# All three branch gates as Strassen products with the tokens stationary and 512 weight columns moving

## Chip, cores and metric

The kernel runs on one core of a Trainium2 chip. The metric is the device time of one execution in microseconds, the median of three runs.

## What is computed

One layer of a streaming encoder on 512 tokens of width 1024, all in float32. The change lies between the attention branches and the output projection:

```python
proj = u @ w_in[l]            # u = rmsnorm(h), 512 x 1024
(gq, gk, gv, gg, ga, fq, fk, fv, ff, mq, gates) = split_cols(proj, PROJ_SIZES)
...
y_gla = o_gla.reshape(B, S, GLA_V) @ w_gla_o[l]
...
y_fox = o_fox.reshape(B, S, FOX_W) @ w_fox_o[l]
...
y_mem = o_mem.reshape(B, S, MEM_W) @ w_mem_o[l]
gt = jax.nn.sigmoid(gates.reshape(B, S, N_BRANCH, D))
merged = gt[:, :, 0] * y_gla + gt[:, :, 1] * y_fox + gt[:, :, 2] * y_mem
h = h + merged @ w_out[l]
```

Each gate is a product of 512 x 1024 by 1024 x 1024, each branch output one of 512 x 512 by 512 x 1024. Behind them stand the projection by w_out and a squared-ReLU MLP of width 4096.

## The kernel before

**Precision.** Every float32 operand is split into a high and a low part, and a product is three matmuls (`mm3`, L169 to L172): high x high, high x low, low x high. The weights come as chunks of 128x1024 (512 KB) from the array `wst`; `load_w` issues the load on SP into one of three buffers named raw, `split_w` casts it on ACT (hi, L160) and subtracts on DVE (lo, L161), three buffers each. On a matmul line the trace names first what is written, then its two operands.

**Order.** The instructions of PE stand in the order in which the code is written. Independent PE work is interleaved by `weave`: after each step of a stage's own list it takes units, one `mm3` each, from generators that fill the gaps, in proportion to the step's share. Where `in_order()` or `issue_after` stand, the order of ACT, DVE and SP is the written one, too; elsewhere a scheduler sets it.

**Stages.** Front (u, the memory keys and values), then the fox stage (forgetting attention, 96 filler units: projections for gla), the mem stage (cross attention, 64 filler units: `fox_out`, which holds four of the eight tiles of the fox gate and the eight tiles of the fox output), the gla stage (64 filler units: `gla_g`, then `fox_late`, the other four tiles of the fox gate), then the gates of mem and gla by `gate_group`, the projection by w_out, the MLP.

**The fox gate before** is a plain product in feature layout: a tile is 128 channels by 512 tokens, weights stationary, 512 tokens moving, 8 x `mm3` a tile. `acc[j]`, eight tiles of 128 channels by 512 tokens, collects the merged branches.

**mem and gla before** use Strassen's scheme in Winograd's form: 7 products for a 2 x 2 block product in place of 8. The blocks A11 to A22 are u (tokens 0 to 255 or 256 to 511, by the two halves of the inputs). A `gate_group` computes 512 channels by 512 tokens: each product takes a chunk of weights, stationary, and 256 tokens of u or of a sum of u's blocks, moving: 24 matmuls 256 wide. The sums of the weight blocks are built in the tiles wb: two loads on SP (L1066, L1067), and more blocks added on top of them by accumulating DMAs from GpSimd (`plus`, L1073). The sums of u's blocks are made on DVE (`u_sum`, `lefts_1`, `lefts_2`) and split into S1 to S4 (f0, f1, f2 and the half of uhl that is no longer read). PSUM products are combined in the ct tiles (`take`), a tanh on ACT gives the gate, `merge` multiplies by the branch output on DVE (L1129) and adds to acc on GpSimd (L1130). In the group with `last` set, the merged tile is split at once into mh and ml for w_out (L1133).

## Time and profile before

| | |
|---|---|
| time, median of 3 runs | 808.15 us (808.0 to 808.75) |
| span of the profiled execution | 806.1 us |
| chain that ended last | PE 96%, DMA 2% |
| chunk casts on ACT, L160, 128x1024 | 61 from raw, mean 1050 ns; 19 from wb, mean 1049 ns |
| chunk splits on DVE, L161, 128x1024 | 61 from raw, mean 1308 ns; 19 from wb, mean 1283 ns |
| DMA | 161.29 MB, mean 200 GB/s |
| ACT's waits for a wb tile's DMA | 18.5 us in 7 times |

The profiled execution stands 2.05 us below the median. A row of a group reads: line, engine, operation, what is written <- what is read with its shape, count, busy time, mean of one. In a timeline a row begins with its start and its duration in us; a matmul's duration overlaps the next one's, so rates are read from starts. In a table of windows each engine's busy time stands with its number of instructions, then PE's granted clock, the share of time in which the DMA engines were busy, and GB/s.

### The profile page before, as it was taken

The numbers are of one execution on the slowest core, as the hardware profiler recorded it, in microseconds if no ns is written. First come the engines' busy times: TensorE is split into PE (matmuls) and PEld (weight loads), VectorE is DVE, ScalarE is ACT, GpSimd is POOL, SyncE is SP. The second block draws the span as 40 slices with busy tenths as digits, with TensorE's granted clock in tenths as the row PEclk, the third lists the DMA queues.
The fourth block names the chain that finished last, engine by engine and source line by source line (L and its number), as shares of the span: only waits on it lengthen the run. The fifth ranks groups of instructions, "written<-read, shape, count | busy, mean of one in ns | idle before, by whom it ended". The sixth has DMA issues, their size and how long they took to land.

```text
span 806.1 us, 12359 instructions
## 1 busy us (share of the span) xinstructions
PE 797.7 (99%) x4703; PEld 699.4 (87%) x4703; DVE 602.2 (75%) x941; ACT 444.0 (55%) x714; POOL 107.2 (13%) x136
## 2 busy tenths in 40 slices
PE   9999999999999999999999999999999999999996
PEld 7788888888888888999999889988998899889985
DVE  6877878456455677877567558788798779978897
ACT  7867555443344334444354446874667366647764
POOL 0000010011101121143144100011001100100011
PEclk9999999999999999999999999999999999999998
DMA  9355665688788877758758823898758966896644
GB/s 355 141 160 165 188 169 183 206 229 254 206 255 260 213 233 200 187 136 209 197 143 236 262 78 131 282 249 216 246 169 197 222 211 174 187 262 214 167 81 131
DMA packets 39628, 161.29 MB, mean 200 GB/s; under 512 B 4752, under 2 KB 5456, under 8 KB 37200
## 3 DMA queue, kind: packets, MB, share of 16 engines
q1 hardware_dynamic: 28432, 98.34, 34.7%
q0 software_dynamic: 9776, 58.20, 34.6%
q10 hardware_dynamic: 1360, 3.96, 1.5%
q8 instruction: 37, 0.61, 0.3%
q14 instruction: 23, 0.19, 0.1%
HBM read 158.35 MB, written 35.68 MB: 241 GB/s over the span
## 4 chain that ended last, share of the span: by engine, by line
PE 96%; DMA 2%; DVE 0%; ACT 0%; SPq 0%; issue 0%; POOLq 0%; DVEq 0%; POOL 0%; ACTq 0%
PE mm L170 17%; PE mm L171 17%; PE mm L172 17%; PE mm L1276 16%; PE a L171 6%; PE a L170 6%; PE a L172 6%; PE mm L1605 3%; PE mm L1606 1%; DMA xt<-in_xT_dram 1%; PE mm L611 1%; DMA mem_s<-in_memT_dram 1%; PE a L404 1%; PE a L664 1%; PE a L702 1%; PE a L701 1%
## 5 line engine op out<-in xcount | busy, mean ns | idle before, releaser
L161 DVE TENSOR_TENSOR wlo<-raw,whi 128x1024 fp32r<-128x1024 f32 x61 | 79.7, 1308 | 55.8 <-ACT whi L160 55.6
L170 PE MATMUL mm<-uhl,whi 128*128 128x512 f32 (+1 forms) x336 | 119.6, 356 | 0.0
L172 PE MATMUL mm<-uhl,wlo 128*128 128x512 f32 (+1 forms) x336 | 117.5, 350 | 0.0
L171 PE MATMUL mm<-uhl,whi 128*128 128x512 f32 (+1 forms) x336 | 117.3, 349 | 0.0
L160 ACT CAST whi<-raw 128x1024 fp32r<-128x1024 f32 x61 | 64.1, 1050 | 85.5 <-PE mm L171 44.0
L1336 DVE TENSOR_TENSOR lo<-raw,hi 128x1024 fp32r<-128x1024 f32 x52 | 63.5, 1223 | 14.8 <-ACT hi L1335 14.7
L1335 ACT CAST hi<-raw 128x1024 fp32r<-128x1024 f32 x52 | 54.4, 1048 | 36.0 <-PE mm L1276 16.2
L170 PEld LDWEIGHTS mm<-uhl,whi 128*128 128x128 f32 x336 | 63.6, 189 | 9.2 <-issue 1.4
L172 PEld LDWEIGHTS mm<-uhl,wlo 128*128 128x128 f32 x336 | 63.6, 189 | 8.5
L171 PEld LDWEIGHTS mm<-uhl,whi 128*128 128x128 f32 x336 | 63.7, 190 | 7.6
L1276 PE MATMUL mm<-u,hi 128*128 128x256 f32 x384 | 65.1, 283 | 0.0
L1655 POOL DMA_DIRECT2D b<-in_wst_dram x30 | 25.6, 855 | 262.5 <-DVE lo L1336 134.3
L1276 PEld LDWEIGHTS mm<-u,hi 128*128 128x128 f32 x384 | 56.8, 191 | 0.3
L170 PE MATMUL mm<-hi,ch 128*128 128x512 f32 (+1 forms) x132 | 50.9, 386 | 0.0
L171 PE MATMUL mm<-lo,ch 128*128 128x512 f32 (+1 forms) x132 | 50.9, 386 | 0.0
L172 PE MATMUL mm<-hi,cl 128*128 128x512 f32 (+1 forms) x132 | 50.9, 386 | 0.0
L1276 PE MATMUL mm<-u2s,hi 128*128 128x256 f32 x288 | 47.6, 283 | 0.0
L1276 PE MATMUL mm<-u,lo 128*128 128x256 f32 x192 | 47.5, 283 | 0.0
L1335 ACT CAST hi<-b 128x1024 fp32r<-128x1024 f32 x26 | 27.2, 1048 | 29.6 <-PE mm L172 20.2
L1276 PEld LDWEIGHTS mm<-u2s,hi 128*128 128x128 f32 x288 | 41.8, 192 | 0.3
L1336 DVE TENSOR_TENSOR lo<-b,hi 128x1024 fp32r<-128x1024 f32 x26 | 31.7, 1224 | 11.0 <-ACT hi L1335 11.0
L161 DVE TENSOR_TENSOR wlo<-wb,whi 128x1024 fp32r<-128x1024 f32 x19 | 24.4, 1283 | 20.7 <-ACT whi L160 20.7
(448 smaller groups left out, 2104.5 us busy)
## 6 DMA issues: line engine op xcount, KB each, us to landing
raw<-in_wst_dram SPq DMA_DIRECT2D x113, 512.0 KB
raw<-T SPq DMA_DIRECT2D x32, 512.0 KB
b<-in_wst_dram POOLq DMA_DIRECT2D x32, 512.0 KB, 5.7
T<-in_wst_dram POOLq DMA_DIRECT2D x12, 1024.0 KB, 9.1
b<-in_wst_dram SPq DMA_DIRECT2D x16, 512.0 KB
wb<-in_wst_dram POOLq DMA_DIRECT2D x15, 512.0 KB, 5.4
T<-in_wst_dram POOLq DMA_DIRECT2D x12, 512.0 KB, 6.0
wb<-in_wst_dram SPq DMA_DIRECT2D x8, 512.0 KB
```

Source lines behind the costliest of these rows:

```text
L160: cast = nc.scalar.copy(hi, raw)
L161: low_now[0] = nc.vector.tensor_tensor(lo, raw, f(hi), op=ALU.subtract).ins
L170: nc.tensor.matmul(ps, lh, rh, start=start, stop=False, skip_group_check=on)
L171: nc.tensor.matmul(ps, lh, rl, start=False, stop=False, skip_group_check=on)
L172: nc.tensor.matmul(ps, ll, rh, start=False, stop=stop, skip_group_check=on)
L404: nc.tensor.matmul(ps, x[:, k, sl], w[low][:, kk, :], start=k == low == 0 and x is mxh, stop=k == KT - 1 and low == 1)
L611: nc.tensor.matmul(ps, w[0][:, k, :], u[:, k, :], start=k == 0 and u is uhi, stop=False)
L1276: nc.tensor.matmul(ps[:, a, :], x[:, a, k, :], y[:, s, k, :], start=start, stop=stop, skip_group_check=go is not None)
L1335: split_now[0] = nc.scalar.copy(hi, raw).ins
L1336: split_now[1] = nc.vector.tensor_tensor(lo, raw, f(hi), op=ALU.subtract).ins
L1605: nc.tensor.matmul(ps, wh[:, a, k, :], u[:, :, k, :], start=k == 0, stop=False, skip_group_check=True)
L1655: nc.gpsimd.dma_start(to[i], wst[index["B", q, i, x]], accum_op=ALU.add)
```

## The change

All three gates run by the same scheme, in token layout: a PSUM tile is 128 tokens by 512 channels, the u blocks are stationary and 512 weight columns move. A gate of 1024 x 1024 weights is one Strassen product, its blocks 512 x 512, each block two chunks of 256 rows by 512 columns. The seven products run in the order 1, 2, 5, 3, 6, 7, 4, two slots of 12 matmuls each; products 1, 6, 7, 4 go on adding in one pair of PSUM tiles, 5 and 3 in another. The code lists slots and what each slot issues on the other engines (`at`), with each chunk's cast and split two slots ahead of its matmuls (`high`, `low`). The three branch outputs are in token layout, too: fox's go straight into acc (now four tiles of 128 tokens by 1024 channels), mem's into ymem, gla's stay in PSUM (Y slots). The merged tile is turned to feature layout for w_out by 32 transposes on PE (`turn`). The fox gate leaves the mem and gla stages; the fillers there are now the gg projections, gla_k(1), gla_q(1) and the outputs, and the sums of u stand in the mem stage.

```diff
-    for j in range(KT):
-        L.append(("T", "w_in", OFF["gate_fox"] + P * j))
-        if j % 2 == 0:
-            L.append(("O", "w_fox_o", j // 2))
-    for g, o in (("gate_mem", "w_mem_o"), ("gate_gla", "w_gla_o")):
-        for i in range(2):
-            L += [("W", g, i, b) for b in ("11", "12", "21", "22")]
-            L += [("O", o, 2 * i + 1), ("O", o, 2 * i)]
+    for g, o in (("gate_fox", "w_fox_o"), ("gate_mem", "w_mem_o"), ("gate_gla", "w_gla_o")):
+        L += [("N", "w_in", 2 * j, OFF[g] + 512 * c) for c in range(2) for j in range(4)]
+        L += [("N", o, 2 * j, 512 * c) for c in range(2) for j in range(2)]
...
-        weave([partial(fn, i) for fn, i, _ in steps], 96, gla_k(0), fox_pair(2), fox_pair(3), gla_k(1), gla_q(0), gla_q(1), gvg,
+        weave([partial(fn, i) for fn, i, _ in steps], 80, fox_pair(2), gla_k(0), fox_pair(3), gla_q(0), gvg,
...
-    acc = [mp.tile([P, S], F32, name=f"acc{j}") for j in range(KT)]
+    acc = [mp.tile([P, D], F32, name=f"acc{t}") for t in range(NT)]
...
+    def outputs(wo, oh, ol, to):
+
+        for c in range(2):
+            ws = [[x.rearrange("p (k c) -> p k c", k=2) for x in get_w(("N", wo, 2 * j, 512 * c))] for j in range(2)]
+            for t in range(NT):
+                ps = mmt()
+                sl = slice(t * P, t * P + P)
+                for k in range(4):
+                    mm3(ps, oh[k][:, sl], ol[k][:, sl], ws[k // 2][0][:, k % 2, :], ws[k // 2][1][:, k % 2, :], k == 0, k == 3)
+                    if k == 3:
+                        nc.scalar.copy(half_of(to[t], c), ps)
+                    yield
...
+    def u_sum(n):
+
+        x = xsum[n] = xsp.tile([P, 4, 256], F32, tag=f"x{n}", name=f"x{n}")
+        if n == 1:
+            nc.vector.tensor_tensor(x, A21[0], A22[0], op=ALU.subtract)
+            nc.vector.tensor_tensor(x, x, A21[1], op=ALU.add)
+            nc.vector.tensor_tensor(x, x, A22[1], op=ALU.subtract)
+        else:
+            nc.vector.tensor_tensor(x, xsum[1], A11[0], op=ALU.subtract)
+            nc.vector.tensor_tensor(x, x, A11[1], op=ALU.subtract)
...
-        Q, A, T, V_ = (lambda i: run(mem_q(i))), mem_scores, mem_turn, mem_values
-        steps = [(Q, 1), (A, 0), (Q, 2), (T, 0), (A, 1), (V_, 0), (Q, 3), (T, 1), (A, 2), (V_, 1), (T, 2), (A, 3), (V_, 2),
-                 (T, 3), (V_, 3)]
-        weave([partial(*st) for st in steps], 64, fox_out())
+        Q, A, T, V_, U = (lambda i: run(mem_q(i))), mem_scores, mem_turn, mem_values, u_sum
+        steps = [(Q, 1, 0), (A, 0, 4), (Q, 2, 4), (T, 0, 2), (A, 1, 2), (V_, 0, 0), (Q, 3, 2), (T, 1, 3), (A, 2, 5), (V_, 1, 5),
+                 (T, 2, 4), (U, 1, 0), (A, 3, 6), (V_, 2, 5), (U, 2, 0), (T, 3, 6), (V_, 3, 0)]
+        weave([partial(fn, i) for fn, i, _ in steps], 48, gla_g(0, mp, "th"), gla_g(1, mp, "th"),
+              outputs("w_fox_o", ofh, ofl, acc), shares=[n for *_, n in steps])
+    ymp = omst.enter_context(pool("ymem", side="right"))
+    ymem = [ymp.tile([P, D], F32, name=f"ymem{t}") for t in range(NT)]
...
+    def gate_key(g, b, n):
+
+        kh, ch = BLOCK[{1: "11", 2: "21", 3: "22"}.get(b, b)]
+        return "N", "w_in", 2 * (2 * kh + n), OFF[g] + 512 * ch
...
+        def gate_ready(n):
...
-            (u_sum, (3,), 0), (gla_turn, (2,), 3), (gate_ready, ("11",), 0), (gate_ready, ("21",), 0), (gla_turn, (3,), 3))
-        weave([partial(fn, *a) for fn, a, _ in steps], 64, *[gla_g(j) for j in range(4)], fox_late(), shares=[n for *_, n in steps])
+            (gla_values, (0,), 0), (gla_scores, (1,), 8), (gla_turn, (0,), 0), (gla_turn, (1,), 4), (gla_values, (1,), 10),
+            (gate_ready, (0,), 0), (gla_turn, (2,), 6), (gate_ready, (1,), 0), (gla_turn, (3,), 0))
+        weave([partial(fn, *a) for fn, a, _ in steps], 64, gla_k(1), gla_q(1), gla_g(2, lp, "og"),
+              outputs("w_mem_o", omh, oml, ymem), gla_g(3, lp, "og"), shares=[n for *_, n in steps])
...
+        GATES = ("gate_fox", "gate_mem", "gate_gla")
+        ORDER = (1, 2, 5, 3, 6, 7, 4)
+        slots = []
+        for g in range(3):
+            for n in ORDER:
+                if g == 2 and n == 4:
+                    slots += [("Y", 1, 0), ("Y", 1, 1)]
+                slots += [(g, n, 0), (g, n, 1)]
+        slots += [("Y", 0, 0), ("Y", 0, 1)] + [("O", 0, j) for j in (2, 3, 0, 1)]
+        at_slot = {k: i for i, k in enumerate(slots)}
...
+        def load_sum(g, n, other):
+            nc.sync.dma_start(sum_tile(g, n, other), wst[index[gate_key(GATES[g], "12" if other else "11", n)]])
+
+        def plus(g, n, other, b):
+            nc.gpsimd.dma_start(sum_tile(g, n, other), wst[index[gate_key(GATES[g], b, n)]], accum_op=ALU.add)
+
+        def source(key):
+            g, n, c = key
+            return raws[key] if key in raws else sum_tile(g, c, n == 7)
+
+        def high(key):
+            hi, lo = ws[key] = [wp.tile([P, 1024], F32R, tag=x, name=nm(x)) for x in ("hi", "lo")]
+            next_sum(nc.scalar.copy(hi, source(key)).ins)
+
+        def low(key):
+            hi, lo = ws[key]
+            nc.vector.tensor_tensor(lo, source(key), f(hi), op=ALU.subtract)
+            if key[0] not in ("Y", "O") and key[1] in (1, 5, 6) and key[:2] != (0, 1):
+                plus(key[0], key[2], 0, {1: "12", 5: "22", 6: "21"}[key[1]])
+
+        def mms(key):
+            g, n, c = key
+            wh, wl = (x.rearrange("p (k c) -> p k c", k=2) for x in ws[key])
+            uh, ul = GATE[n]
+            if c == 0 and n in (1, 2, 5):
+                cur[n] = [(at_ if n == 2 else mmt)() for _ in range(2)]
+            ps = cur[{1: 1, 6: 1, 7: 1, 4: 1, 2: 2, 5: 5, 3: 5}[n]]
+            for t in range(2):
+                for k in range(2):
+                    kk = 2 * c + k
+                    mm3(ps[t], uh[:, kk, spans[t]], ul[:, kk, spans[t]], wh[:, k, :], wl[:, k, :], n in (1, 2, 5) and kk == 0,
+                        kk == 3, True)
...
+        def evac(ps):
+            tt = pool_.tile([P, S], F32, tag=tag, name=nm("tt"))
+            nc.scalar.activation(tt, ps, AF.Tanh, scale=0.5)
+            nc.vector.scalar_tensor_tensor(sg[j], tt, 1.0, ps, op0=ALU.add, op1=ALU.mult)
+            nc.vector.tensor_scalar(sg[j], sg[j], ghead[:, j:j + 1], 0.5, op0=ALU.mult, op1=ALU.mult)
+        return proj(OFF["gg"] + P * j, evac)
+
+    xsum = {}
+    A11, A12, A21, A22 = ([f(t[:, 4 * k:4 * k + 4, 256 * i:256 * i + 256]) for t in (uhi, ulo)] for i in range(2) for k in range(2))
+
...
+        def merge(g, i, c, ys=None):
+            for t in (2 * i, 2 * i + 1):
+                x, a = th[g, i, c][:, t % 2], half_of(acc[t], c)
+                if g == 0:
+                    nc.vector.scalar_tensor_tensor(a, x, 1.0, a, op0=ALU.add, op1=ALU.mult)
+                else:
+                    nc.vector.scalar_tensor_tensor(x, x, 1.0, half_of(ymem[t], c), op0=ALU.add, op1=ALU.mult)
+                    merged[0] = nc.gpsimd.tensor_tensor(a, a, x, op=ALU.add).ins
...
+        def turn(t, c):
+            pt = (at_ if c else mmt)([P, 4, P])
+            for k in range(4):
+                nc.tensor.transpose(pt[:, k, :], half_of(acc[t], c)[:, k * P:(k + 1) * P], ident)
+            h, l = (x[:, 4 * c:4 * c + 4, spans[t]] for x in (mh, ml))
+            nc.scalar.mul(h, pt, 0.5)
+            nc.vector.scalar_tensor_tensor(l, pt, 0.5, f(h), op0=ALU.mult, op1=ALU.subtract)
+
+        def sum_four():
+            vec(xsum[1], xsum[2], A12[0])
+            vec(xsum[1], xsum[1], A12[1])
+
+        def sum_three():
+            x = xsum[2]
+            nc.vector.scalar_tensor_tensor(x, x, -1.0, A22[0], op0=ALU.mult, op1=ALU.subtract)
+            vec(x, x, A22[1], ALU.subtract)
...
+        for g in range(3):
+            if g:
+                for n in range(2):
+                    at((g - 1, 7, 1), load_sum, g, n, 0, shift=-1)
+                    at((g - 1, 4, 1), load_sum, g, n, 1, shift=-1)
+                    at((g - 1, 4, 1), plus, g, n, 1, "22", shift=-1)
+            for n in (2, 3):
+                for c in range(2):
+                    at((g, n, c), get, (g, n, c), shift=max(-5, -at_slot[g, n, c]))
...
+        at((0, 1, 1), vec, sum_tile(0, 0, 0), sum_tile(0, 0, 0), sum_tile(0, 0, 1), shift=-1)
+        at((0, 1, 1), plus, 0, 0, 1, "22", shift=-1)
+        at((0, 1, 1), left, S1, xsum[1], shift=-1)
+        at((0, 1, 1), vec, sum_tile(0, 1, 0), sum_tile(0, 1, 0), sum_tile(0, 1, 1))
+        at((0, 1, 1), plus, 0, 1, 1, "22")
+        at((0, 5, 0), sum_four)
+        at((0, 5, 1), left, S4, xsum[1])
+        at((0, 3, 0), left, S2, xsum[2])
+        at((0, 6, 0), sum_three)
+        at((0, 6, 1), left, S3, xsum[2])
...
+        for n in range(2):
+            load_sum(0, n, 0)
+            load_sum(0, n, 1)
+        ws.update({(0, 1, n): w for n, w in enumerate(ready)})
...
+                early = [x for x in before.get(i, []) if x[0] in (get, load_sum, merge)]
+                for fn, args in early:
+                    fn(*args)
+                for j in ([1, 2] if i == 0 else [i + 2]):
+                    if j < len(slots) and slots[j] not in ws:
+                        high(slots[j])
+                        low(slots[j])
+                for fn, args in before.get(i, []):
+                    if (fn, args) not in early:
+                        fn(*args)
```

**SP, the loads at the start of the gates.** raw are single chunks, wb the tiles in which weight blocks are summed. Before:

```order
L153 DMA raw_492_3081<-in_wst_dram 128x1024
L153 DMA raw_495_3088<-in_wst_dram 128x1024
L1066 DMA wb_508_3133<-in_wst_dram 128x1024
L1067 DMA wb_509_3134<-in_wst_dram 128x1024
L153 DMA raw_512_3139<-in_wst_dram 128x1024
L153 DMA raw_528_3330<-in_wst_dram 128x1024
```

After (raw_487 is the fourth chunk of the gate, and takes the buffer of raw_477, the first):

```order
L148 DMA raw_477_2993<-in_wst_dram 128x1024
L148 DMA raw_478_2995<-in_wst_dram 128x1024
L148 DMA raw_483_3020<-in_wst_dram 128x1024
L148 DMA raw_487_3044<-in_wst_dram 128x1024
L1064 DMA wb_473_2985<-in_wst_dram 128x1024
L1064 DMA wb_475_2987<-in_wst_dram 128x1024
L1064 DMA wb_474_2986<-in_wst_dram 128x1024
L1064 DMA wb_476_2988<-in_wst_dram 128x1024
```

Two wb loads stood among loads of chunks; now four stand in a row behind raw_487.

On DVE this is what follows the fourth chunk's raw there (after; lo_480 and lo_485 are the splits of product 2's two chunks, sg3 and og3 belong to the gla stage):

```order
L1079 TENSOR_TENSOR lo_480_2998<-raw_477_2993,hi_479_2997 128x1024
L788 SCALAR_TENSOR_TENSOR sg3_119<-tt_460_2950,mm_454_2909 128x512
L789 TENSOR_SCALAR sg3_119<-sg3_119,cols_s_74 128x512
L982 TENSOR_TENSOR og_465_2966<-a_464_2961,sg3_119 128x512
L219 TENSOR_TENSOR og3_2431<-og_465_2966,og3_2431 128x512
L1039 TENSOR_TENSOR wb_473_2985<-wb_473_2985,wb_475_2987 128x1024
L1036 TENSOR_TENSOR f0l_468_2980<-x1_2272,f0h_467_2979 128x1024
L1079 TENSOR_TENSOR lo_485_3023<-raw_478_2995,hi_484_3022 128x1024
```

The sum of the first two wb tiles and S1's low part stand ahead of lo_485 now.

**DVE and ACT, fox's products 2 and 3 (before: mem's first group).** wb are sums of weight chunks, x1 and x2 sums of u's blocks, f0l, f1l, f2l the low parts of S1, S2, S4, ct the combined products. DVE before:

```order
L1082 TENSOR_TENSOR wb_508_3133<-wb_508_3133,wb_509_3134 128x1024
L1047 TENSOR_TENSOR f0l_503_3128<-x1_2955,f0h_502_3127 128x1024
L224 TENSOR_TENSOR uhl_100<-x3_3059,uhl_100 128x4x256
L1082 TENSOR_TENSOR ct_510_3135<-ct_510_3135,mm_516_3177 128x2x256
L161 TENSOR_TENSOR wlo_520_3231<-wb_508_3133,whi_519_3230 128x1024
L1053 TENSOR_TENSOR x1_2955<-uhl_100,x1_2955 128x1024
L1054 TENSOR_TENSOR x1_2955<-x1_2955,uhl_100 128x1024
L161 TENSOR_TENSOR wlo_523_3266<-wb_509_3134,whi_522_3265 128x1024
```

DVE after, from the combination of product 2 on:

```order
L1039 TENSOR_TENSOR ct_486_3041<-ct_486_3041,a_490_3052 128x512
L1039 TENSOR_TENSOR ct_486_3041<-ct_486_3041,a_491_3053 128x512
L1079 TENSOR_TENSOR lo_495_3087<-raw_483_3020,hi_494_3086 128x1024
L1039 TENSOR_TENSOR x1_2272<-x2_2369,uhl_100 128x1024
L1039 TENSOR_TENSOR x1_2272<-x1_2272,uhl_100 128x1024
L1139 SCALAR_TENSOR_TENSOR acc0_1806<-ct_486_3041,acc0_1806 128x512
L1139 SCALAR_TENSOR_TENSOR acc1_1807<-ct_486_3041,acc1_1807 128x512
L1079 TENSOR_TENSOR lo_499_3109<-raw_487_3044,hi_498_3108 128x1024
L1036 TENSOR_TENSOR f2l_472_2984<-x1_2272,f2h_471_2983 128x1024
```

ACT after, at the same place:

```order
L1075 CAST hi_492_3066<-wb_474_2986 128x1024
L1100 ACTIVATE ct_486_3041<-ct_486_3041 128x1024
L1075 CAST hi_494_3086<-raw_483_3020 128x1024
L1075 CAST hi_498_3108<-raw_487_3044 128x1024
L1035 CAST f2h_471_2983<-x1_2272 128x1024
```

Behind the sum with product 2 stand now a chunk's split, the two sums for S4, two merges into acc, another chunk's split and S4's low part, and on ACT the tanh of 1024 columns stands ahead of the casts of both chunks of product 3 and of S4.

More of the change, by code (lines that the diff above doesn't have):

```diff
@@ L806, in fox_late, with half_of @@
-    def fox_late():
-        for j in range(4, KT):
-            yield from fox_gate(j, lambda th: nc.vector.scalar_tensor_tensor(acc[j], th, 1.0, acc[j], op0=ALU.add, op1=ALU.mult))
+    def half_of(t, c):
+        return t[:, 512 * c:512 * c + 512]
+    def outputs(wo, oh, ol, to):
[9 more added lines that the diff above has]
+                    yield
@@ L1202, in hybrid_block @@
-        gate_group("gate_mem", "w_mem_o", omh, oml, 0, ready=ready)
-        gate_group("gate_mem", "w_mem_o", omh, oml, 1)
-        omst.close()
-        mhp = late.enter_context(pool("mhl"))
-        mh = mhp.tile([P, KT, S], F32R, name="mh")
-        ml = mhp.tile([P, KT, S], F32R, name="ml")
-        gate_group("gate_gla", "w_gla_o", ogh, ogl, 0, last=(mh, ml))
-        gate_group("gate_gla", "w_gla_o", ogh, ogl, 1, last=(mh, ml))
-        late_on.append(1)
-        hN = [h_tile(t, "h") for t in range(NT)]
@@ new lines, in merge @@
+        def merge(g, i, c, ys=None):
[6 more added lines that the diff above has]
+                    merged[0] = nc.gpsimd.tensor_tensor(a, a, x, op=ALU.add).ins
+        wide = {}
@@ new lines, in last_merge @@
+        def last_merge(c):
+            for t in range(NT):
+                x, a = th[2, t // 2, c][:, t % 2], half_of(acc[t], c)
+                nc.vector.scalar_tensor_tensor(x, x, 1.0, wide["Y", c][t], op0=ALU.add, op1=ALU.mult)
+                vec(a, a, x)
+        def turn(t, c):
[5 more added lines that the diff above has]
+            nc.vector.scalar_tensor_tensor(l, pt, 0.5, f(h), op0=ALU.mult, op1=ALU.subtract)
@@ L1240, in hybrid_block @@
+        u2j = up.tile([P, 2, 4, 4, 256], F32R, tag="uhl", name="u2")
+        u2 = [u2j[:, i] for i in range(2)]
+        mst.close()
+        unp.append(late.enter_context(pool("un")))
+        bp = ctx.enter_context(pool("blocks", side="right"))
+        b11, b12 = ([bp.tile([P, 1024], F32, name=f"b{n}{i}") for i in range(2)] for n in ("11", "12"))
+        plain = {(0, 0): b11[0], (0, 1): b11[1], (1, 0): b12[0], (1, 1): b12[1]}
         own_n = [0]
@@ L1249, in out_w @@
             return own_w(key) if key[2] < 4 else get_w(key)
-        run(gN([("N", "w_out", 2 * j, 0) for j in range(4)], of(mh, ml), NT, at_, res_evac(0)))
+        for t in range(NT):
+            res_evac(0)(t, wide["O", 0][t])
         c1 = gN([("N", "w_out", 2 * j, 512) for j in range(4)], of(mh, ml), NT, mmt, res_evac(1), tail=4, get=out_w)
```

323 lines of the change are left out of this document (109 added, 214 removed).

## The prediction

> **What bounds the kernel now.** I read the busy times first, then the chain that ended last, then PE's own waits, then the stages of the change.
>
> ```profile
> PE 797.7 (99%) x4703; PEld 699.4 (87%) x4703; DVE 602.2 (75%) x941; ACT 444.0 (55%) x714; POOL 107.2 (13%) x136
> PE a L302 <- DVE warm L299: 1.2, 1, 1.2
> PE a L430 <- DVE xsq L350: 0.2, 1, 0.2
> ```
>
> PE is busy for 797.7 of 806.1 us, and the second and third line are all the waits that the trace finds for it: 1.4 us, both at the start. So a product taken off PE is worth its full time, and a wait put in front of PE costs its full time: there is no idle time to hide it in.
>
> ```profile
> core 0: us, PE busy (x) PEld busy (x) DVE busy (x) ACT busy (x) POOL busy (x), PEclk, DMA share, GB/s
> 314.00:345.00 31.00, 31.00 (x216) 28.86 (x215) 26.50 (x29) 16.48 (x19) 5.11 (x6) 1.00 0.70 178
> 345.00:376.00 31.00, 31.00 (x217) 29.07 (x216) 21.95 (x21) 13.39 (x16) 11.32 (x10) 1.00 0.74 179
> 376.00:408.00 32.00, 32.00 (x223) 29.92 (x223) 20.57 (x23) 14.05 (x18) 9.55 (x8) 1.00 0.73 188
> 408.00:438.50 30.50, 30.50 (x214) 28.60 (x213) 21.24 (x24) 14.44 (x19) 10.76 (x10) 1.00 0.65 193
> ```
>
> These are the four Strassen groups (mem, mem, gla, gla). PE is full in each at a granted clock of 1.00. DVE is at 26.5 of 31 us (85%) in the first, where the sums of u are made, and near 70% in the others. That first group is kept dense by the order of its work, not by spare DVE time; it is there that the change must be read.
>
> **What PE gains.** Pitches, from starts of neighbouring matmuls:
>
> ```profile
> 183.37 0.39 PE L170 MATMUL mm<-uhl,whi 128*128 128x512 f32 x1
> 184.05 0.39 PE L170 MATMUL mm<-uhl,whi 128*128 128x512 f32 x1
> 314.01 0.28 PE L170 MATMUL mm<-uhl,whi 128*128 128x256 f32 x1
> 319.76 0.40 PE L170 MATMUL a<-omh,whi 128*128 128x512 f32 x1
> 308.05 0.40 PE L172 MATMUL mm<-uhl,wlo 128*128 128x512 f32 x1
> 308.29 0.60 PE L973 MATMUL a<-cst_s,on 128*128 128x128 f32 x4
> 308.64 0.48 PE L170 MATMUL mm<-uhl,whi 128*128 128x512 f32 x1
> 308.96 0.40 PE L171 MATMUL mm<-uhl,whi 128*128 128x512 f32 x1
> ```
>
> Three 512-wide matmuls take 184.05 − 183.37 = 0.68, so 0.2267 each. From 314.01 to 319.76 stand 48 of 256 wide: 0.1198 each, 0.0065 more than half. Removed: fox, 8 x 8 x 3 = 192 wide ones, 43.5 us; mem and gla, 4 groups x 7 products x 24 = 672 narrow ones, 80.5 us. Added: 3 gates x 7 products x 24 = 504 wide ones, 114.3 us. That is 9.8 us less; most of it, 43.5 − 38.1 = 5.4, is the eighth product that fox saves, 4.3 the width. The projections by w_fox_o, w_mem_o, w_gla_o and w_out keep their counts. New are 32 transposes that turn the merged tile, 8 groups of four: a group takes 0.35, and the matmul behind it starts 0.1 later than it would (0.32 instead of 0.23), so 8 x 0.45 = 3.6 us. **If PE stays dense: −9.8 + 3.6 = −6.2 us**, a span of 799.9.
>
> The Trainium skill, TensorE: Matmul & The Clock Gate, section Back-to-back issue gap, gives an isolated gap of N/2.4 + 2.5 ns, 216 for 512 columns and 109 for 256. By it the exchange would save an estimated 6.0 us, not 9.8, and so speaks against the width; the rows above have 227 and 120 ns, and they decide.
>
> **What the change asks of the other engines.** A product's half is now one "slot": 12 wide matmuls, 12 x 0.2267 = 2.72 us, with one chunk of 128x1024 weights cast on ACT and split on DVE two slots ahead. ORDER is 1, 2, 5, 3, 6, 7, 4. S0 is the start of slot 0; slot n starts at 2.72 n. A triple takes the weights' low part second and that of u third, so these are due 0.23 and 0.45 behind the start of their slot.
>
> ```profile
> 314.77 1.04 ACT L160 CAST whi<-raw 128x1024 fp32r<-128x1024 f32 x1
> 315.70 1.05 ACT L1046 CAST f0h<-x 128x1024 fp32r<-128x1024 f32 x1
> 317.60 0.59 ACT L1098 COPY ct<-mm 128x512 f32<-128x512 f32 x1
> 321.10 0.63 ACT L1085 ACTIVATE ct<-ct 128x512 f32<-128x512 f32 x1 [1.82 <-DVE ct L1082]
> 316.98 1.22 DVE L1082 TENSOR_TENSOR wb<-wb,wb 128x1024 f32<-128x1024 f32 x1
> 318.11 1.22 DVE L1047 TENSOR_TENSOR f0l<-x,f0h 128x1024 fp32r<-128x1024 f32 x1
> 320.38 0.68 DVE L1082 TENSOR_TENSOR ct<-ct,mm 128x512 f32<-128x512 f32 x1
> 320.98 1.22 DVE L161 TENSOR_TENSOR wlo<-wb,whi 128x1024 fp32r<-128x1024 f32 x1
> 322.12 1.22 DVE L1053 TENSOR_TENSOR x<-uhl,x 128x1024 f32<-128x1024 f32 x1
> 323.37 1.22 DVE L1054 TENSOR_TENSOR x<-x,uhl 128x1024 f32<-128x1024 f32 x1
> ```
>
> ACT takes 1.05 for 1024 columns (next one 0.95 later), 0.6 for 512. DVE takes 1.22 (1.13 apart, 1.25 where the second needs the first) and 0.68 (0.60 apart). A tanh of 1024 columns is not in the trace; between two of 0.63 and one cast I take 1.05. In the fox gate DVE has 14 splits, 10 sums and lefts of 1024 and 12 operations of 512: 24 x 1.13 + 12 x 0.60 = 34.3 us of 38.1, 90%. Throughput fits; the chains do not, since ACT and DVE run in the written order:
>
> **Step D, late sums.** In the new SP order the raw of the gate's fourth chunk, raw_487, stands ahead of the four loads of the sum tiles. It reuses the buffer that the split lo_480 reads, whose cast needs the buffer that the last matmul ahead of S0 frees: 0.2 + 1.05 + 1.22, so SP goes on near S0 + 2.6.
>
> ```profile
> 284.66 0.42 SPq L1066 DMA_DIRECT2D wb<-in_wst_dram  x1
> 285.14 0.55 SPq L1067 DMA_DIRECT2D wb<-in_wst_dram  x1
> 442.10 12.01 SPq L153 DMA_DIRECT2D raw<-in_wst_dram  x5
> 445.78 1.05 ACT L223 CAST f0h<-raw 128x1024 fp32r<-128x1024 f32 x1 [1.89 <-DMA raw<-in_wst_dram]
> 455.00:460.00 5.00, 5.00 (x24) 4.14 (x23) 1.34 (x2) 2.10 (x2) 0.52 (x1) 1.00 1.02 387
> 440.00:445.00 5.00, 5.00 (x24) 4.14 (x23) 4.47 (x4) 1.27 (x2) 3.71 (x3) 1.00 0.96 247
> wb<-in_wst_dram POOLq DMA_DIRECT2D x15, 512.0 KB, 5.4
> ```
>
> Before, these loads went out at 284.66, 29 us ahead of the first product at 314.01. A 512 KB load lands 445.78 − 442.10 = 3.7 us after its issue, and each further one 1.35 later at 387 GB/s, 2.1 at 247. The first pair, third in line, lands at 2.6 + 3.7 + 2.7 = S0 + 9.0 at best. On DVE its sum, then f0l, then lo_485 follow: 3 x 1.13 + 0.1 gives 12.5. lo_485 is due in slot 3 at 8.16 + 0.23 = 8.4. **Stall 4.1.** With 5.4 for the first load, as the accumulating ones have it, and 247 GB/s it is 7.3. With loads in time DVE would come from lo_480 at 2.5 over five operations of 512 columns left by the gla stage (3.2) and the same three to 9.1: stall 0.7.
>
> The Trainium skill, DMA: Bandwidth & Descriptors, section Anatomy of one DMA, has 2.0 us plus bytes at 436 GB/s, an estimated 5.6 us for three such loads against the 6.4 that I take from the rows; the forecast would be 0.8 lower by it. No row shows loads queued in that state.
>
> **Step A, product 3 of fox.** Its left side S4 is summed only now. From the end of product 2 (start of slot 4): lag 0.25, second add 0.68, tanh 1.05, cast hi_494 0.95 behind it, split lo_495 1.22, the two sums of S4 2.5, two merges 1.2, lo_499 1.13, f2l 1.13: 10.1. The third matmul of slot 6 is due 5.44 + 0.45 = 5.9 later. **Stall 4.2**; 5.4 if DVE comes in one operation late.
>
> **Step B, product 7 of fox.** From the start of slot 8, which frees hi's buffer: 0.2 + 1.05 cast hi_505, 1.22 lo_506, 2.5 for the two sums of S3, 1.13 lo_508, 1.13 low part of S3: 7.2, due at 5.9. **Stall 1.3.**
>
> **Step C, the two gate borders.** Product 1 of mem starts in the PSUM tiles that the tanhs of fox's product 4 read, and follows that product directly: lag 0.25, 0.63 and a start give a stall of 1.0; the second tile is read while the first fills. The same holds at gla's border, and there the merges' POOL additions run beside the splits:
>
> ```profile
> 343.98 2.85 POOL L1130 TENSOR_TENSOR acc<-acc,ct 128x512 f32<-128x512 f32 x2
> 344.82 4.24 DVE L161 TENSOR_TENSOR wlo<-raw,whi 128x1024 fp32r<-128x1024 f32 x2
> 348.98 1.27 DVE L1129 SCALAR_TENSOR_TENSOR ct<-ct,a 128x512 f32<-128x512 f32 x2
> ```
>
> Two splits took 4.24 beside them instead of 1.13 + 1.22 = 2.35, 1.9 more, which is later than the tanhs' 1.0. **Together 2.9**; the tanhs alone 2.0, and 0 if the matmuls end earlier than their modelled records say.
>
> **At nothing:** the fillers moved between the fox, mem and gla stages, the sums of u in the mem stage, the 8 plain copies of projections, the merge and turn behind gla. Their cover is woven PE work (0.68 per unit) and Y slots of 5.44; without it they cost 0 to 3 us in all.
>
> **Sum.** 806.1 − 6.2 + 4.1 + 4.2 + 1.3 + 2.9 = 812.4. The median of the runs is 808.15, 2.05 above the profiled span; with that, 814.4. **I predict 814.4.**
>
> **The rivals.**
> - *Dense PE (0.15, faster).* The gate stage holds because ACT and DVE run further ahead than my walk has it, above all if the sum tiles and S4 are ready a few us earlier. It needs stalls under 6.2 − 1.6 = 4.6 in all to show as faster; with none it gives 799.9 + 2.05 = 802. For it speaks that before has no such stall at 85% DVE; against it that step A alone starts from a PE result and costs 4.2 in rows of this trace.
> - *Only the chains (0.10).* Loads land in time and POOL costs nothing: 0.7 + 4.2 + 1.3 + 2.0 = 8.2, so 810; with nothing at the borders 6.2, which eats the gain: 808.
> - *All of it slow (0.20).* D 7.3, A 5.4, B 1.3, C 2.9, earlier stages 3: 19.9, so 806.1 − 6.2 + 19.9 + 2.05 = 822. DMA shares of 0.65 to 0.74 before, with 8 accumulating loads per 38 us now instead of 4 per 31, speak for it.
> - *The exchange is no gain (0.05).* Tokens stationary have a wider pitch than weights stationary; nothing of the 4.3 comes: 818.7.
>
> The forecast with its steps keeps 0.50.
>
> **How the numbers follow.** A measurement tells 0.2%, 1.6 us, from no change. Faster: the dense case and a sliver of the second, 0.17; within: 0.07; slower: 0.76. The range takes in the chains-only case at its lower bound, 808, with 2 for a DVE that is one or two operations ahead of the walk in A, and the slow case above: 806 to 823. It leaves out the dense case and a tail above, under 2 in 10.
>
> **What would show it.** PE's waits in the new trace: on lo_485's split or f0l in slot 3 with the sum tile's DMA behind it (D), on S4's cast and low split in slot 6 (A), on S3 in slot 10 (B), on the tanhs in slots 14 and 28 (C); 504 wide matmuls at 0.227. No waits there makes the prediction wrong by their size; waits in the fox, mem or gla attention stages would mean that the fillers run out, which I priced at nothing.

## The result, and the profile after

After takes 840.64 us (median of 4 runs, 839.94 to 841.76) against 808.08 for before in the same session (807.47 to 808.75): 1.0403 times as long, with an interval of 1.0388 to 1.0418. The forecast was 814.4, its range 806 to 823. The sign came as forecast; the size did not.

The page of after, in the order of the prediction: the span, the busy times, then PE and its granted clock in 40 slices.

```profile
span 840.0 us, 11701 instructions
PE 803.6 (96%) x4375; PEld 684.2 (81%) x4375; DVE 606.1 (72%) x945; ACT 461.5 (55%) x733; POOL 102.5 (12%) x135
PE   9999999999999948898999999999999999999996
PEclk9999999999999978999999999999999999999998
```

PE was busy for 797.7 of 806.1 us; now it is for 803.6 of 840.0. Its idle time went from 8.4 to 36.4 us, 28.0 more. Its busy time, which should have fallen by 6.2 to 791.5, rose by 12.1 over that. So 33.9 = −6.2 + 28.0 + 12.1. Most of both lies in the slices from the 15th to the 19th, in the three gates.

PE's waits in the gates of after: what waited and on which line, for what, then us in total, times, and the longest.

```profile
PE a L166 <- DVE lo L1079: 11.6, 1, 11.6
PE mm L165 <- DVE ct L1039: 5.6, 2, 3.3
PE mm L165 <- ACT ct L1117: 4.3, 2, 2.4
PE mm L165 <- ACT hi L1075: 1.2, 1, 1.2
PE mm L167 <- DVE f2l L1036: 1.2, 1, 1.2
PE mm L165 <- ACT ct L1121: 0.9, 1, 0.9
PE mm L166 <- DVE lo L1079: 0.8, 1, 0.8
```

That is 25.6 us of the 28.0. Ahead of the gates one wait is new, 0.9 for a PSUM tile in the gla stage (line L949), a place that the forecast priced at nothing. The timeline of PE tells where each stands (start, duration, instruction, and in brackets the idle time before it and its releaser):

```profile
314.38 0.80 PE L166 MATMUL a<-lo,uhl 128*128 128x512 f32 x1 [11.58 <-DVE lo L1079]
314.97 0.63 PE L167 MATMUL a<-hi,uhl 128*128 128x512 f32 x1
315.40 0.63 PE L165 MATMUL a<-hi,uhl 128*128 128x512 f32 x1
...
327.46 0.50 PE L165 MATMUL mm<-hi,f2h 128*128 128x512 f32 x1 [2.42 <-ACT ct L1117]
...
329.38 0.50 PE L167 MATMUL mm<-hi,f2l 128*128 128x512 f32 x1 [1.18 <-DVE f2l L1036]
...
342.62 0.50 PE L165 MATMUL mm<-hi,uhl 128*128 128x512 f32 x1 [0.92 <-ACT ct L1121]
...
350.91 0.47 PE L165 MATMUL mm<-hi,uhl 128*128 128x512 f32 x1 [2.24 <-DVE ct L1039]
...
368.70 0.50 PE L165 MATMUL mm<-hi,f0h 128*128 128x512 f32 x1 [1.19 <-ACT hi L1075]
369.96 0.50 PE L166 MATMUL mm<-lo,f0h 128*128 128x512 f32 x1 [0.76 <-DVE lo L1079]
...
397.49 0.47 PE L165 MATMUL mm<-hi,uhl 128*128 128x512 f32 x1 [3.35 <-DVE ct L1039]
...
423.05 0.50 PE L165 MATMUL mm<-hi,f2h 128*128 128x512 f32 x1 [1.85 <-ACT ct L1117]
```

The first is D's place (product 2 of fox, its second chunk's split lo). 327.46 and 329.38 are A (product 3: the copy's buffer, then S4's low part), 342.62 is B's place, product 7 of fox. The other four were priced nowhere. At 350.91 and 397.49 product 4 of fox and of mem starts in the PSUM tiles in which product 7 was accumulated, and goes on adding there, so it waits until DVE has read product 7 out of them. At 368.70 and 369.96 product 5 of mem waits for the cast and split of a weight sum whose accumulating DMA landed late, and at 423.05 product 3 of gla for a chain that begins with another such landing.

The three rows from 314.38 show the second term: starts are 0.43 apart where dense matmuls are 0.227. The windows of the four stretches behind the longest waits (busy times by engine, granted clock, DMA share, GB/s):

```profile
314.40:319.70 5.30, 5.30 (x13) 4.14 (x14) 4.24 (x5) 1.04 (x1) 3.46 (x4) 0.50 0.59 114
329.40:333.40 4.00, 4.00 (x11) 3.14 (x12) 2.19 (x2) 0.39 (x1) 0.86 (x1) 0.57 0.96 166
370.00:374.40 4.40, 4.40 (x12) 3.46 (x13) 2.42 (x3) 1.77 (x2) 1.71 (x2) 0.61 0.64 104
397.50:401.70 4.20, 4.20 (x12) 3.29 (x13) 2.14 (x3) 1.99 (x2) 1.63 (x3) 0.59 0.72 257
```

The clock was granted to about half there, and 1 − clock times the length gives 2.7 + 1.7 + 1.7 + 1.7 = 7.8 us of the 12.1, counted by the page as busy.

Most of the other 4.3 stands in late starts. From S0, the start of the gates at 294.14, to the first transpose at 457.20 stand 558 wide matmuls. They take 163.1 us, where dense ones take 558 x 0.2267 = 126.5. Of the 36.6 lost the brackets hold 25.6 and the clock 7.8, so 3.2 are left. A bracket counts from the end of the matmul before, which is a modelled one, 0.39 behind its start, though dense starts are only 0.227 apart; and the first matmul behind a wait is followed late (342.62, then 342.95). So each wait costs PE some 0.3 us more than its bracket says. 1.1 of the 12.1 stay open.

Why D was so long shows on DVE, POOL and SP (timelines of after, same columns) and in one window:

```profile
296.46 2.43 SPq L1064 DMA_DIRECT2D wb<-in_wst_dram  x1
298.99 0.38 SPq L1064 DMA_DIRECT2D wb<-in_wst_dram  x1
...
300.08 0.82 POOL L126 DMA_DIRECT2D T<-in_wst_dram  x1 [9.67 <-ACT f0h L1035]
311.74 0.52 POOL L128 DMA_DIRECT2D T<-T  x1 [10.85 <-DMA T<-in_wst_dram]
312.60 0.88 POOL L1067 DMA_DIRECT2D wb<-in_wst_dram  x1 [0.34 <-issue]
...
310.82 1.23 DVE L1039 TENSOR_TENSOR wb<-wb,wb 128x1024 f32<-128x1024 f32 x1 [11.47 <-DMA wb<-in_wst_dram]
...
296.46:310.82 14.36, 6.34 (x28) 4.90 (x27) 2.07 (x4) 3.60 (x5) 0.82 (x1) 0.83 0.88 282
```

SP issued the first of the four loads of sum tiles at 296.46, as forecast (S0 is 294.1, so S0 + 2.4; I had 2.6). That issue took 2.43 us (0.43 in k6 below), so the second load of the pair went out only at 298.99. The pair let DVE go on at 310.82, 14.4 us after the first issue and not 6.4. In between the DMA engines are 88% busy, among other things with T: transfers of 1024 KB that sum weight blocks for the MLP. The trace's own records of landings and packets show what that did: fifteen of the second load's sixteen parts had landed by 305.51, the last one at 310.73; in these 5 us the packets of the T step issued at 300.08 (8192 bytes, 0.63 us each) alternate with those of the loads (4096 bytes, 0.17). T's steps are issued by a pacing helper, one step per weight cast; the change has fewer casts ahead of the gates, so its last steps now fall into them. GpSimd's queue takes its DMAs in order: the step at 311.74 waits 10.85 us for the one before it to land, and the first addition stands behind it.

### The profile page after: what moved, and what is told of

Read it like the earlier page. It is cut to its first block, busy times and chain, and to the rows that moved or that the text cites. A ratio compares the mean times of both kernels' runs of the same rounds, so it can differ in the third digit from the quotient of the medians.

```text
span 840.0 us, 11701 instructions
## 1 busy us (share of the span) xinstructions
PE 803.6 (96%) x4375; PEld 684.2 (81%) x4375; DVE 606.1 (72%) x945; ACT 461.5 (55%) x733; POOL 102.5 (12%) x135
## 3 DMA queue, kind: packets, MB, share of 16 engines
q1 hardware_dynamic: 28576, 98.86, 32.8%
## 4 chain that ended last, share of the span: by engine, by line
PE 83%; DMA 6%; DVE 5%; ACT 3%; issue 2%; POOL 0%; POOLq 0%; DVEq 0%; SPq 0%; ACTq 0%
PE mm L165 15%; PE mm L166 14%; PE mm L167 14%; PE mm L1316 13%; PE a L166 4%; PE a L167 4%; PE a L165 4%; DMA wb<-in_wst_dram 3%; PE mm L1645 3%; PE mm L386 1%; PE mm L1646 1%; PE a L399 1%; DMA b<-in_wst_dram 1%; DVE lo L1079 1%; ACT hi L1075 1%
## 5 line engine op out<-in xcount | busy, mean ns | idle before, releaser
L156 DVE TENSOR_TENSOR wlo<-raw,whi 128x1024 fp32r<-128x1024 f32 x38 | 46.5, 1224 | 39.6 <-ACT whi L155 39.5
L1376 DVE TENSOR_TENSOR lo<-raw,hi 128x1024 fp32r<-128x1024 f32 x52 | 63.5, 1223 | 13.9 <-ACT hi L1375 13.8
L155 ACT CAST whi<-raw 128x1024 fp32r<-128x1024 f32 x38 | 40.0, 1051 | 48.3 <-PE mm L166 14.9
L1079 DVE TENSOR_TENSOR lo<-wb,hi 128x1024 fp32r<-128x1024 f32 x28 | 38.6, 1382 | 37.4 <-ACT hi L1075 37.4
L165 PE MATMUL mm<-uhl,whi 128*128 128x512 f32 x144 | 57.8, 402 | 0.0
L167 PE MATMUL mm<-uhl,wlo 128*128 128x512 f32 x144 | 56.2, 391 | 0.0
L166 PE MATMUL mm<-uhl,whi 128*128 128x512 f32 x144 | 56.2, 390 | 0.0
L1075 ACT CAST hi<-wb 128x1024 fp32r<-128x1024 f32 x28 | 29.2, 1048 | 45.8 <-PE mm L167 17.4
L1079 DVE TENSOR_TENSOR lo<-raw,hi 128x1024 fp32r<-128x1024 f32 x20 | 26.5, 1332 | 15.7 <-ACT hi L1075 15.7
L166 PE MATMUL a<-lo,ch 128*128 128x512 f32 (+1 forms) x96 | 37.1, 387 | 0.3 <-DVE lo L1433 0.3
```

Of the source, the lines that this page charges most:

```text
L155: cast = nc.scalar.copy(hi, raw)
L156: low_now[0] = nc.vector.tensor_tensor(lo, raw, f(hi), op=ALU.subtract).ins
L165: nc.tensor.matmul(ps, lh, rh, start=start, stop=False, skip_group_check=on)
L166: nc.tensor.matmul(ps, lh, rl, start=False, stop=False, skip_group_check=on)
L167: nc.tensor.matmul(ps, ll, rh, start=False, stop=stop, skip_group_check=on)
L1075: next_sum(nc.scalar.copy(hi, source(key)).ins)
```

## The experiments

Three theories were on the table: (L) late and crowded transfers at the head of the gates, (R) reads of PSUM that hold the next product, and (P) a price of the additions or of the clock that no order removes. Ratios are against before; differences below are against after's 840.64 unless another run is named.

**One part of the order at a time.** The four loads ahead of raw_487:

```diff
-        for n in range(2):
-            load_sum(0, n, 0)
-            load_sum(0, n, 1)
         with in_order():
+            for n in range(2):
+                load_sum(0, n, 0)
+                load_sum(0, n, 1)
```

> The changed kernel with one move: the four loads of fox's sum tiles are issued on SP ahead of the gate's chunk loads (raw_477 to raw_487) instead of behind them. If the late issue alone makes the 11.58 us wait ahead of slot 3, that wait falls to 0 to 1 us, the 12 matmuls at half clock behind it (2.6 us) go, and the time falls from 840.6 by 11 to 14 us, to about 828. If it is the transfers of T that hold the loads up, wherever they stand, the wait stays above 5 us and the time above 833.

831.9 us, 1.0292 [1.0276, 1.0307]: 8.7 less, not the 11 to 14 expected. D's 11.58 is gone, and the waits on the copy L1117 rise from 4.3 to 7.3: 3.8 at A's place, where it had been 2.4, and 1.9 at product 3 of mem, where there was none. So D needs the late issue of the loads, behind T's steps, and A's chain was partly hidden behind it.

The steps of T sooner (one more step at five casts of the earlier stages):

```diff
-        for to, src, add_ in islice(sums[len(late_on)], 1 + (len(late_on) == 1)):
+        for to, src, add_ in islice(sums[len(late_on)], 1 + (len(late_on) == 1) + (n in (17, 20, 23, 26, 29))):
```

> The changed kernel with one move: five of the T transfers (sums of w_ff1 blocks in DRAM, issued from GpSimd, one for each weight cast) are issued as second ones with earlier casts, so that the last of them stands ahead of the gates instead of at 300, 312 and 318 us. If the late issue alone makes the first wait, it stays between 9 and 12 us and the time within 3 us of 840.6. If these transfers crowd the loads, the landing falls from 14 us to 6 to 9, the wait from 11.6 to 3 to 6, and the time by 6 to 9 us, to about 833.

836.16 us, 1.034 [1.0322, 1.0357]. From PE's waits of this run:

```profile
PE a L166 <- DVE lo L1079: 4.9, 1, 4.9
PE a L914 <- DVE kn L902: 3.5, 1, 3.5
```

D falls from 11.6 to 4.9, and T now crowds the gla stage, where 3.5 appear that were not there; the gain is 4.5, not the 6 to 9 expected. Sums S2 to S4 made one to three slots sooner, and product 1 of mem in PSUM tiles of its own:

```diff
-        at((0, 5, 0), sum_four)
-        at((0, 5, 1), left, S4, xsum[1])
...
+        at((0, 1, 1), sum_four)
+        at((0, 2, 0), left, S4, xsum[1])
...
-                cur[n] = [(at_ if n == 2 else mmt)() for _ in range(2)]
+                cur[n] = [(at_ if n == 2 or (g, n) == (1, 1) else mmt)() for _ in range(2)]
```

> The changed kernel with one move: the sums of u's blocks for products 3 and 7 (S4, S3) and their splits stand two to three slots earlier in the order of DVE and ACT, where DVE waits anyway. If the chains of steps A and B are what PE waits for in slots 6 and 10, these waits (2.42, 1.18 and 0.92 us) and the slow clock behind them (1.7) go: 840.6 falls by 4 to 6 us, to about 835. If the weight chunks of the same slots are just as late, less than 2 us are gained.

> The changed kernel with one move: the first product chain of the mem gate takes the two PSUM tiles of the other pool that are free, so it need not wait for the tanhs of fox's product 4. If the PSUM tiles make the border wait of 2.24 us, it goes and the time falls by about 2 us, to 838.5. If the chunk for that slot is as late, or if the next wait (on a sum tile's accumulation) grows by the same amount, the time stays within 1 us of 840.6.

840.35 and 840.51 us, 1.0402 [1.0384, 1.0419] and 1.0403 [1.0384, 1.0422]: nothing. With S4 sooner the copy of product 5 holds product 3 for 2.3 all the same: on ACT it stands behind three casts and the tanh of product 2, and that tanh needs DVE to have combined product 2. With other tiles at the border the waits of 2.2 and 3.4 for L1039 remain; the border (step C) costs nothing, the read of product 7 does.

**Parts together.** f1 is e1 and e2; f2 also moves the loads and additions for product 7's sum tiles (blocks 12 and 22) some slots later; f3 adds e3.

> Both moves of e1_loads_first and e2_T_sooner. If late issue and crowding are two parts of one delay, the first wait is gone and the time is 826 to 829, 4 to 6 us under e1 (831.9). If the transfers of T only crowd loads that go out late, it stays within 1.5 us of e1.

> f1 with one more move: the loads and accumulations for product 7's sum tiles (blocks 12 and 22), needed last, are issued four to six slots later, apart from those for product 5. If the gates' accumulations are late because ten transfers of 512 KB are asked for in four slots (11 us), the landing of the accumulations falls from a median near 8 us to near 6, the waits at products 5 and 3 of mem and gla (2 us each) go, and the time falls 3 to 6 us under f1. If PE waits there because of the order on ACT and DVE, it stays within 1.5 us of f1.

> f2 with the sums of u earlier, as in e3_sums_sooner. In e3 the move gave nothing since late weight sums took over. If that was the cover, it gives now 3 to 5 us under f2, its waits on f2h, f2l and ACT's copy at product 3 of fox gone; if DVE has no room in the fox gate anyway, under 1.5 us.

830.81, 830.5 and 830.16 us (1.0278 [1.0261, 1.0295], 1.0278 [1.025, 1.0306], 1.0288 [1.0254, 1.0322]). The two moves don't add up (8.7 + 4.5 were 13.2; it is 9.8), and further ones of this kind bring nothing that can be told, where f2 was expected to give 3 to 6 and f3 another 3 to 5: the 5.6 of L1039 stand in all three.

**The additions left out.** What `plus` issues is dropped, once in f1 and once in after itself:

```diff
-            nc.gpsimd.dma_start(sum_tile(g, n, other), wst[index[gate_key(GATES[g], b, n)]], accum_op=ALU.add)
+            pass
```

> f1 with every accumulating DMA of the gates left out (the sum tiles hold their first block only; blocks 12, 22 and 21 are not added). If the weight sums' transfers are the rest of the loss, the time falls to 812 or less, about where the chains of ACT and DVE alone leave it. If the written order of ACT and DVE and the read of a chained PSUM tile between two products make the loss, it stays above 820.

> The changed kernel with nothing moved and every accumulating DMA of the gates left out. Against 840.6 and k2 this parts the loss: if the transfers make most of it whatever the order, 820 or less; if late loads and order make most of it, above 828.

825.77 us (1.021 [1.0188, 1.0233]), 5.0 less than f1; and 836.02 (1.0342 [1.03, 1.0383]), 4.6 less than after. D stands at 11.6 in k5 as in after, so the additions aren't its cause. The DMA queue that carries them, from the pages of f1 and then of f4 (packets, MB, share of 16 engines):

```profile
q0 software_dynamic: 10784, 61.87, 34.9%
```

```profile
q0 software_dynamic: 7616, 50.34, 27.4%
```

0.349 x 830.7 − 0.274 x 823.9 = 64 us of all 16 engines for 22 additions of 512 KB: 2.9 each.

**The reads of PSUM first.** Product 2 is combined only behind product 5, the merges come later, and at the end of fox's and of mem's gate one split is issued between DVE's two reads of product 7, not ahead of them:

```diff
+                    while after_read:
+                        low(after_read.pop())
...
-                    at((g, n, 1), merge, g, i, c, shift=2)
+                    at((g, n, 1), merge, g, i, c, shift={2: 5, 6: 3, 7: 3, 4: 3}[n])
...
-                        low(slots[j])
+                        if key[1:] == (7, 1) and key[0] in (0, 1):
+                            after_read.append(slots[j])
+                        else:
+                            low(slots[j])
...
```

> The changed kernel with one move: the instructions that read a chained PSUM tile, which the next product goes on adding to, stand ahead of others on ACT and DVE: product 5's copies ahead of product 2's tanh, product 7's subtractions ahead of a split, the merges one to three slots later. If PE waits because the next product may not write a tile before it is read, the waits on L1117, L1121 and L1039 (2.42, 0.92, 2.24, 3.35, 1.85 us) shrink to under 3 us in all and the time falls by 6 to 9 us from 840.6 with the slow clock behind them, though the 11.6 us at slot 3 stay. If late weight sums set these places, under 2 us are gained.

836.25 us, 1.0344 [1.032, 1.0368]: 4.4 less, not 6 to 9. The waits of 2.24, 3.35 and 1.85 are mostly gone, and 3.5 appears at product 7 of fox, where it had been 0.9. With e1's loads and the sums for S4 and S3 one slot sooner it is h2; h3 puts the "22" additions behind those that product 5 needs.

> Loads first on SP (as e1), the sums for S4 and S3 one or two slots earlier, and the reads first (as h1). If the three causes (late loads, the chain over S4, the reads between chained products) are the loss and each is cured, PE waits under 6 us in the gates, the clock stays at 1.0, and the time is 810 to 816. If DVE's work in the fox gate (90% of it) is too much in whatever order, the waits come up elsewhere and the time stays above 822.

> h2 with block 22 for product 7 asked for behind the additions that product 5 needs, where GpSimd's queue stood waiting for a load to land (14.2 us before the issue at 351.23 in the changed kernel). If that queue makes product 5's chunks late in mem and gla, h3 is 2 to 5 us under h2; if DMA bandwidth does, within 1 us.

827.81 and 829.66 us, 1.0233 [1.0213, 1.0254] and 1.0258 [1.0242, 1.0274]: h2 is far from its 810 to 816, and h3 gains nothing on it. Of h2, GpSimd's queue and PE:

```profile
312.65 0.52 POOL L128 DMA_DIRECT2D T<-T  x1 [9.96 <-ACT ct L1117]
313.16 2.69 POOL L1067 DMA_DIRECT2D wb<-in_wst_dram  x3
...
325.93 0.80 PE L165 MATMUL mm<-hi,f1h 128*128 128x512 f32 x1 [8.65 <-ACT f1h L1035]
```

Here the wait has only moved on: three additions stand behind a step of T that could not go until 312.65, and product 6 waits 8.65 us.

**All four.** k1 is h2 with the steps of T sooner, at n = 12, 14, 16, 18 and 20, so that none falls into the gates; k2 is k1 without the additions.

> h2 with the T transfers sooner (five second ones with earlier casts than in e2). In h2 one wait of 8.65 us stood ahead of product 6 of fox, behind an addition into a sum tile that GpSimd issued only after a T transfer it had waited 9.96 us for. If the T transfers make that wait, by the queue or by the DMA engines, it falls under 2 us and the time from 827.8 to 817 to 821. If the additions of the gate alone fill the DMA engines, it stays above 5 us and the time above 824.

> k1 with every accumulating DMA of the gates left out (blocks 12, 22 and 21 are not added to the sum tiles). With neither the written order nor the weight sums in the way, PE should be dense in the gates and the arithmetic of the prediction hold: 802 to 807. If something that I have not seen costs PE time in the new form of the products, it stays above 812.

821.33 us, 1.0168 [1.0137, 1.0198], and 817.06, 1.0111 [1.0096, 1.0126]. The 8.65 is gone, and k1 is the best order that I found that computes the whole, 19.3 below after and still slower than before. Its waits and those of k2, the longest of each:

```profile
PE a L697 <- DVE PTl L219: 2.8, 1, 2.8
PE mm L165 <- ACT hi L1075: 1.9, 1, 1.9
```

```profile
PE a L697 <- DVE PTl L219: 2.5, 1, 2.5
PE mm L165 <- DVE ct L1039: 1.2, 2, 1.0
...
129.13:132.55 3.42, 3.42 (x16) 3.12 (x16) 3.06 (x6) 1.17 (x2) 1.29 (x2) 0.50 0.73 175
297.87:499.00 201.13, 196.81 (x909) 160.38 (x908) 138.32 (x158) 100.19 (x132) 23.01 (x20) 1.00 0.39 130
```

With no addition and T out of the way the clock is granted in full in the gates (the last row, with w_out and part of the MLP), the DMA share is 0.39, and no wait in the gates is over about 1.0. k2 was expected far lower, at 802 to 807. Its span of 816.4 is 16.5 above the dense 799.9: 9.9 of it is PE idle (816.4 − 798.1, less 8.4), 6.6 is PE busy over 791.5. The 2.5 at L697, which h2 does not have, is T's price in an earlier stage; 3.4 us at half clock follow it, 1.7 of the 6.6. Another 3.8 are late starts as in after: from 298.22 to the first transpose at 432.82 the 558 matmuls take 134.6 us and not 126.5, and of these 8.1 the brackets hold 4.3. 1.1 stay open.

**T behind the gates.** The last steps of T given to the part that runs behind the gates: alone (k6), with h2's order (k7), and with the merges' additions on DVE in place of GpSimd (k8).

```diff
-    sums = [islice(sum_ops(), *x) for x in ((32,), (32, 36), (36, None))]
+    sums = [islice(sum_ops(), *x) for x in ((27,), (27, 36), (36, None))]
...
-                    merged[0] = nc.gpsimd.tensor_tensor(a, a, x, op=ALU.add).ins
+                    merged[0] = nc.vector.tensor_tensor(a, a, x, op=ALU.add).ins
```

> The changed kernel with one move: the last five T transfers that run ahead of or in the fox gate (they serve the MLP's last quarter) are held back until the end of the gla gate. In e2 the transfers went ahead of the gates and took 5 us there (waits in the gla stage). If T's transfers cost the fox gate 7.4 us, as e2's gate stage says, this gains 7 to 9 us on 840.6, to about 832.5, with no wait ahead of the gates. If the late issue alone makes the first wait, it stays within 2 us of 840.6.

> h2 with the T transfers held back as in k6_T_behind. k1, which sent them sooner, stands at 821.3 with 4 us lost ahead of the gates. If that loss is T's alone, this gives 815 to 818; if the additions fill the DMA engines anyway, 821 or more.

> k7_all_T_behind with the merge additions of the mem gate on DVE instead of GpSimd. Beside a GpSimd addition a DVE split takes up to 3.5 us instead of 1.23. If that sharing makes the waits of 0.4 to 1.3 us at gla's first slots, they go and 2 to 4 us are gained; if the eight additions cost DVE as much as they save, within 1 us.

840.95, 827.3 and 825.83 us (1.0413 [1.0396, 1.043], 1.0242 [1.0227, 1.0257], 1.0223 [1.0201, 1.0245]). k7 stays above its 815 to 818, in the range of its second case (821 or more), whose cause this does not show; k8 can't be told from it. k6 is the run to read: two places on PE, ACT between them, and two windows.

```profile
306.36 0.50 PE L166 MATMUL a<-lo,uhl 128*128 128x512 f32 x1 [3.91 <-DVE lo L1079]
...
469.30 1.05 ACT L1075 CAST hi<-raw 128x1024 fp32r<-128x1024 f32 x1 [16.13 <-DMA raw<-in_wst_dram]
...
475.74 0.79 PE L165 MATMUL a<-hi,mh 128*128 128x512 f32 x1 [2.29 <-ACT mh L1173]
...
450.00:470.00 20.00, 19.87 (x97) 16.16 (x96) 7.77 (x11) 2.63 (x4) 2.14 (x3) 1.00 1.02 323
476.00:482.00 6.00, 5.86 (x12) 3.22 (x12) 4.07 (x6) 3.30 (x5) 0.77 (x1) 0.51 0.72 244
```

Without T at their head the gates show D at 3.91, against the forecast's 4.1. The gain is given back 160 us later: T and the loads of that stage fill the engines to 1.02 (0.74 in after's same window), a chunk lands so late that ACT stands 16.13 us, and a wait with half clock behind it follows. T has to be somewhere, and no place tried was free.

## Why the prediction went wrong

The profiled span is 840.0 where the sum gave 812.4, 27.6 more. By the steps:

| step | forecast | in the trace |
|---|---|---|
| D, late sums | 4.1 (0.7 to 7.3) | 11.58 |
| A, product 3 of fox | 4.2 (to 5.4) | 2.42 + 1.18 = 3.60 |
| B, product 7 of fox | 1.3 | 0.92 |
| C, gate borders | 2.9 (0 to 2.9) | 0 |
| DVE's reads of product 7 ahead of product 4 | not priced | 2.24 + 3.35 = 5.59 |
| additions that land late (product 5 of mem, 3 of gla) | not priced | 1.95 + 1.85 = 3.80 |
| half clock behind waits | not priced | 7.8 |
| late starts behind waits | not priced | 3.2 |

- **The step that failed first is D, in its size.** The mechanism is the one forecast: the place, the engine, and SP's first issue at S0 + 2.4. What was mis-sized is the term "3.7 us after its issue, and each further one 1.35 later": the pair landed at S0 + 16.6 and not at S0 + 9.0. Some 2 us of that is SP's slow first issue, the rest is the last part of the second load, behind T's packets. The 3.7 was also misread. The cast at 445.78 does not read the load of 442.10, but the one before it (before, issues of T and SP):

```profile
436.62 1.67 POOL L131 DMA_DIRECT2D T<-in_wst_dram  x2
438.66 0.33 SPq L153 DMA_DIRECT2D raw<-in_wst_dram  x1
```

  So this load took 7.1 us, beside two steps of T, and with 7.1 the same sum makes D 7.5. I had seen that the additions load the engines more and left it to the slow rival; the steps of T, which the change moves into the gates, I had not followed at all. e2 and k6, which move T in opposite directions, bring D to 4.9 and 3.9. With T away the forecast's 4.1 comes out, but by luck: the wrong pair of rows happened to give about the time of a load without T beside it (3.9 for raw_487 in k6). The missing step is: each paced transfer of a helper moves when the number of its paces ahead of a stage changes.
- **A and B held** in place and near in size, but only in part in kind. At both places PE first waits for ACT's copy out of a PSUM tile that the next product goes on adding to (L1117, L1121). The forecast doesn't have these copies; they come late since they stand behind the casts of S4 and S3. Of A's 3.60 only the 1.18 on f2l is the wait that was named, and in e3, with S4 sooner, 2.26 remain there. A's price also hung on D: with D gone (e1) it is 3.77 + 0.69 = 4.46.
- **C failed.** I priced the tanhs' reads at the border, which e4 shows to cost nothing, and not the reads one product earlier. The change chains product 4 to product 7 in one PSUM tile, so DVE must read product 7 out before product 4 goes on, with splits standing ahead of the read. DVE's timeline in after, ahead of the wait that ends at 397.49:

```profile
394.46 2.29 DVE L1079 TENSOR_TENSOR lo<-wb,hi 128x1024 fp32r<-128x1024 f32 x1
396.67 1.27 DVE L1039 TENSOR_TENSOR ct<-ct,mm 128x512 f32<-128x512 f32 x2
```

  The split takes 2.29 where one takes 1.22 alone, and the two reads of product 7 come behind it. I had such slow splits in the rows beside the merges' additions on GpSimd, and put them at the border. h1, which moves split and merges together, takes most of these waits away; it doesn't tell the two apart.
- **The clock was not in the sum.** The forecast priced each wait by its length. In after 7.8 us more are lost at half clock behind them, and 3.2 in late starts.
- **The −6.2 us** was never seen by itself, but nothing speaks against it: the pitch of 0.227 holds wherever PE is dense, and in k2 PE's busy time is 798.1, which without the 1.7 at half clock and the 3.8 of late starts is 792.6, where the forecast has 791.5.
- **The rivals:** the slow one (822) came nearest and stopped 19 short. It had D at 7.3 and nothing for T, PSUM reads or the clock.

By the runs, of the 32.6 us between after and before about 19 belong to orders (k1: loads first, reads first, sums and T sooner), 4 to 5 to the additions whatever the order (f4, k2, k5). The 9 us that k2 stands above before are T's place, waits of about 1 us each with the late starts behind them, and 1.1 that stay open; they outweigh what the exchange saves.

## What to carry to other kernels

Before pricing a load that a change puts late, list everything that will share its DMA engines and its queue, above all transfers that are paced by counting other instructions: the change moves them without naming them. Where products are chained in PSUM, the read between two of them is part of PE's path, and belongs first in its engine's order. And this kernel, with its busiest engine at 99%, had no free place: most moves here shifted the wait, so add a price for each wait that a fix uncovers, and read it from the starts of the matmuls and not from the bracket. Before taking a load's time from two rows, make sure that the issue and the landing belong to the same load.
